# Gates and log-gate sums of a hybrid decoder step: one block of work cut into seven steps, and the cached sums in two wide matmuls

## The chip, the cores and the metric

One core of one Trainium2 chip runs the whole program. The metric is the device time of one execution in microseconds (us). A profiled execution gives a trace in which every instruction has a start, a length and, where its engine sat idle before it, what ended that idle time. The engines are PE (TensorE), ACT (ScalarE), DVE (VectorE), POOL (GpSimd) and SP, which issues most DMAs here. Each of them takes its instructions in a fixed order.

## The reference, cut to what matters

One layer serves a prompt of 1024 rows and 8 samples of 4 new rows, each sample with 1024 cached rows in 8 pages of 128. All matrices are float32. What bears on the change is the forget-gate side of the second head group (FoX), the branch gates of the first (NSA), and the projections around them:

```python
u = h @ w_in                                    # D = 1024, all head groups' columns side by side
logf = log_sigmoid(f_f + b_fgate)               # (b, t, 8 heads)
gates = sigmoid(g_n.reshape(b, t, KV_NSA, GRP, 3))
# prompt
c = cumsum(logf, axis=1)                        # 1024 rows
# samples
c_past = cumsum(gather_pages(cache_fox_logf, page_table, layer), axis=1)   # 8 samples x 1024 rows x 8 heads
c_new = c_past[:, -1:] + cumsum(logf, axis=1)
# both
logit = q . k * HEAD_DIM ** -0.5 + (cq - ck)    # then a masked softmax over the keys
...
cmp_kv = compress_blocks(kv_c, cmp_pos, w_cmp1, w_cmp2)   # NSA: an MLP over 32-row blocks of the cached rows
```

## The kernel before, in words

The normalised input lies transposed in eight tiles `ht`, split into a high and a low float32r half. A **projection** (`proj`, L227 to L246) makes 128 columns of `u` for all 1056 rows: it loads the weights in four DMAs (`wr`), ACT casts each to `wh` (L82), POOL subtracts to get `wl` (L83), and PE runs 72 matmuls of 352 columns (L243), 24 for each of three column chunks. Each chunk needs one PSUM tile of the tag `fl`, which has **two** buffers, and frees it when ACT or DVE has copied it out: for a q projection that copy is `os` (L509) on ACT.

A **compression chunk** (`cmp_chunk`, L422 to L485) takes two samples' pages (or, as the chunk `(NB,)`, the prompt's own rows in the tiles `cT`): transposes (L440, tags `sc` and `pt`), splits into tiles `X` (ACT L82, DVE L83), 48 matmuls for each of e = 0, 1 (L455, tags `pv` and `sv`; L460 for the prompt), a tanh (L472 on ACT, L473 and L474 on DVE) and a small product (L478). These tags are not `fl`.

`gates_and_sums` (L265 to L363) does the rest, all of it in `fl` tiles:

- L276: the projection for 24 gate and 8 forget columns, 48 matmuls, copied out to `gt`; L284 and L287 turn it to rows (`gf`).
- L291 to L322: tanh for the gates; Abs, Exp and Ln for the log-gates `lf`; seven additions for the prefix `pre` over the prompt's eight row blocks.
- L324, L325, L329: the prompt's cumulative sums, with a triangle of ones (`TRI`) and a full square of ones, copied out to `cn`, then turned and stored (`d_c`).
- L335 gathers the cached log-gates of 64 pages into `lp`; L343 turns them in eight transposes to `lpt`.
- L350 and L351: the cached cumulative sums. For each head, `lpt` of that head against `TRI`, and a 64x64 block matrix (`L64`) against the page totals `tot`, 16 matmuls of 128 columns in two PSUM tiles, then L353 and eight stores to `d_cs` (L355).
- L358 to L363: the sums for the new rows.

The program order around it is set by hand (L542 to L557): it is called once, after the chunk `(2, 3)` and a projection, and is followed by a projection, the chunk `(4, 5)`, two projections, the chunk `(NB,)` and the chunk `(6, 7)`. The framework's scheduler then fixes each engine's order with a model of its own: it may bring an instruction forward when its buffers allow, so the chunks' work, in other tags, stands among the gates' work, and the projections, in the same tag, stand behind it.

Much later `sam_fox` (L1156 to L1233) reads `d_cs` back as the tile `nk`, one DMA for four samples.

Of the kernel before, what the change touches and what calls it, by code (L numbers as in the profile page):

```python
# [25 lines left out]
TA = T + NS  # L26
# [5 lines left out]
      ("L64", 64), ("B64", 32), ("IMP", 16), ("IDX", 14), ("BM", 64), ("CM4", 4), ("WM4", 4), ("DG", 2)]  # L32
# [12 lines left out]
def tile_hymba_step(ctx: ExitStack, tc: tile.TileContext, I: dict, O: dict):  # L45
    nc = tc.nc

    def raw(t, off, dims):
        return bass.AP(tensor=t.tensor, offset=t.offset + off, ap=dims)
# [18 lines left out]
    def mm_tile(tag="fl"):  # L68
        return pst[1].tile([128, 512], F32, name="ps_" + tag, tag=tag, bufs=pst[2][tag])
# [20 lines left out]
    def evac(out, in_, scale=None):  # L90
        ev_n[0] += 1
        if scale is not None or ev_n[0] % 3:
            nc.scalar.activation(out, in_, AF.Copy, scale=1.0 if scale is None else scale)  # L93
        else:
            nc.vector.tensor_copy(out, in_)  # L95
# [39 lines left out]
    d_cs = dram.tile([NB, 8, 1024], F32, name="d_cs")  # L135
# [129 lines left out]
    def gates_and_sums():  # L265
        wg = gpool.tile([128, KD, 32], F32, name="wg")
        nc.sync.dma_start(wg[:, :, 0:24], w_in[:, 1280:1304].rearrange("(k p) c -> p k c", p=128))
        nc.sync.dma_start(wg[:, :, 24:32], w_in[:, 3352:3360].rearrange("(k p) c -> p k c", p=128))
        gt = lp_.tile([128, TA], F32, name="gt", tag="cT", bufs=3)
        for c in range(3):  # L270
            ps = mm_tile()
            s = slice(c * CH, (c + 1) * CH)
            for r in range(4):
                for q in range(4):
                    k = q + 4 * (r // 2)
                    nc.tensor.matmul(ps[32 * q:32 * q + 32, :CH], lhsT=wg[:, k], rhs=HT[k][:, r % 2, s].bitcast(F32),  # L276
                                     start=r == 0, stop=r == 3)
            evac(gt[:, s], ps[:, :CH])
        stk = cst[:, CO["STK"]]
# [17 lines left out]
        bf = gpool.tile([128, 8], F32, name="bf")  # L297
        nc.sync.dma_start(bf, raw(I["b_fgate"], 0, [[0, 128], [1, 8]]))
# [22 lines left out]
        for t in range(1, NT):  # L321
            nc.vector.tensor_add(pre[:, t], pre[:, t - 1], lf[:, t - 1])  # L322
        ps = mm_tile()
# [21 lines left out]
        cp = lp_.tile([128, TA], F32, name="cp", tag="cT", bufs=3)[:64, :1024].rearrange("p (h t) -> p h t", h=8)  # L345
        for h0 in (0, 4):
            ps = mm_tile()
            for h in range(4):
                o = ps[:64, h * 128:(h + 1) * 128]
                nc.tensor.matmul(o, lhsT=lpt[:, h0 + h], rhs=cst[:, CO["TRI"]], start=True, stop=False)  # L350
                nc.tensor.matmul(o, lhsT=cst[:64, CO["L64"]],  # L351
                                 rhs=tot[:, h0 + h:h0 + h + 1].to_broadcast([64, 128]), start=False, stop=True)
            nc.vector.tensor_scalar(cp[:, h0:h0 + 4], ps[:64].rearrange("p (h c) -> p h c", c=128), -1.0, None, op0=OP.mult)  # L353
        for b in range(NB):
            nc.sync.dma_start(d_cs[b].rearrange("h (g c) -> g h c", c=128), cp[b * 8:(b + 1) * 8])  # L355
# [131 lines left out]
    F0, F1, F2, F3, F4, F5 = 2, 1, 1, 2, 0, 0  # L487
# [37 lines left out]
    for e in range(2):  # L525
# [15 lines left out]
        pos.append(pT.rearrange("p (u j) -> p j u", u=2))  # L541
    cmp_chunk((0, 1), pgs)  # L542
    nsa_projections(F0)
# [3 lines left out]
    nsa_projections(F1)  # L547
    pgs = cmp_pages((4, 5))
    gates_and_sums()
    nsa_projections(F2)  # L550
    cmp_chunk((4, 5), pgs)
    nsa_projections(F3)
    pgs = cmp_pages((6, 7))
    cmp_chunk((NB,), None)
    nsa_projections(F4)
    cmp_chunk((6, 7), pgs)
    nsa_projections(F5)  # L557
# [598 lines left out]
    def sam_fox(gq):  # L1156
        bs = [gq * 4 + bl for bl in range(4)]
        nk = sp.tile([128, 1056], F32, name="nk", tag="s_l")[:, :1024]
        nc.sync.dma_start(nk, raw(d_cs, gq * 4 * 8192, [[1024, 32], [0, 4], [1, 1024]]))
# [259 lines left out]
def _consts():  # L1419
# [19 lines left out]
    l = np.zeros((128, 64))  # L1439
    l[:64] = (r[:, None] // 8 == r[None] // 8) & (r[:, None] % 8 < r[None] % 8)  # L1440
    c["L64"] = l
# [57 lines left out]
```

## Time and profile before

| | us |
|---|---|
| median of 3 runs | 1305.86 |
| lowest and highest run | 1299.7 and 1306.3 |
| the profiled execution | 1305.1 |
| its span, first to last instruction | 1303.3 |
| PE busy in it | 1206.6 |
| mean granted clock of TensorE (share of full) | 0.971 |

In the rows further down, PE is the matmul stream; one float32 matmul can show as two records (x2). "PEclk" is the share of TensorE's full clock of 2.4 GHz that was granted in a stretch: 1.00 is 2.4 GHz, 0.50 is 1.2 GHz, and values between are stretches with some of both. A text in brackets at the end of a timeline row is the idle time of the engine just before it and what ended it.

### The profile page before, as it was taken

The numbers are of one execution on the slowest core, as the hardware profiler recorded it, in microseconds if no ns is written. First come the engines' busy times: TensorE is split into PE (matmuls) and PEld (weight loads), VectorE is DVE, ScalarE is ACT, GpSimd is POOL, SyncE is SP. The second block draws the span as 40 slices with busy tenths as digits, with TensorE's granted clock in tenths as the row PEclk, the third lists the DMA queues.
The fourth block names the chain that finished last, engine by engine and source line by source line (L and its number), as shares of the span: only waits on it lengthen the run. The fifth ranks groups of instructions, "written<-read, shape, count | busy, mean of one in ns | idle before, by whom it ended". The sixth has DMA issues, their size and how long they took to land. (4 is left out here: it accounts for less than half of the span.)

```text
span 1303.3 us, 23755 instructions
## 1 busy us (share of the span) xinstructions
PE 1206.6 (93%) x8130; PEld 988.6 (76%) x8130; DVE 667.5 (51%) x2054; ACT 605.6 (46%) x1415; POOL 315.9 (24%) x433
## 2 busy tenths in 40 slices
PE   3899889999999999999889999999999787999998
PEld 3799669998989998989866666664664666877776
DVE  4614542434556566364368677665545746342222
ACT  7624433334455545453357676664555733131121
POOL 2411002022322222221132232222212433222112
PEclk8999969999999999999889999999999988999999
DMA  7434212047332223223552624546645465542221
GB/s 243 131 110 119 77 34 82 20 117 215 88 86 58 78 58 97 59 73 97 183 156 76 195 95 144 165 136 201 208 132 162 142 234 162 173 154 81 70 74 37
DMA packets 142747, 157.07 MB, mean 121 GB/s; under 512 B 16602, under 2 KB 109562, under 8 KB 142434
## 3 DMA queue, kind: packets, MB, share of 16 engines
q1 hardware_dynamic: 141394, 151.10, 37.7%
q10 hardware_dynamic: 1152, 4.19, 0.8%
q8 instruction: 64, 1.05, 0.3%
q14 instruction: 57, 0.47, 0.1%
q0 software_dynamic: 80, 0.26, 0.1%
HBM read 128.33 MB, written 36.38 MB: 126 GB/s over the span
## 5 line engine op out<-in xcount | busy, mean ns | idle before, releaser
L243 PE MATMUL ps_fl<-ht,wh 128*128 128x352 f32 x1440 | 367.0, 328 | 7.4 <-DVE os L498 3.6
L243 PEld LDWEIGHTS ps_fl<-ht,wh 128*128 128x128 f32 x1440 | 256.1, 190 | 12.4 <-DVE os L498 3.9
L243 PE MATMUL ps_fl<-ht,wl 128*128 128x352 f32 x720 | 236.3, 328 | 0.0
L620 ACT ACTIVATE s<-s,m 128x64 f32<-128x64 f32 (+8 forms) x256 | 164.4, 644 | 58.7 <-DVE m L618 55.6
L83 POOL TENSOR_TENSOR wl<-wr,wh 128x256 fp32r<-128x256 f32 x120 | 89.5, 750 | 267.7 <-ACT wh L82 266.7
L623 POOL TENSOR_SCALAR s<-s,rs 128x64 f32<-128x64 f32 (+8 forms) x160 | 93.4, 604 | 232.7 <-DVE rs L981 138.1
L243 PEld LDWEIGHTS ps_fl<-ht,wl 128*128 128x128 f32 x720 | 136.7, 190 | 1.1 <-issue 0.4
L638 PE MATMUL ps_pt<-cst,s 128*128 128x128 f32 x816 | 128.3, 284 | 3.3 <-POOL s L623 0.8
L612 PE MATMUL ps_sc<-kh,q 128*128 128x320 f32 (+12 forms) x304 | 116.4, 387 | 13.1 <-DVE m L618 7.0
L618 DVE CUSTOM_DVE_ANT_0 s<-ps_sc,bias 128x128 f32<-128x128 f32 (+10 forms) x224 | 80.3, 389 | 83.9 <-PE ps_sc L613 22.0
L638 PEld LDWEIGHTS ps_pt<-cst,s 128*128 128x128 f32 x816 | 97.8, 144 | 23.1 <-issue 6.0
L93 ACT ACTIVATE s<-ps_pt 128x512 f32<-128x512 f32 (+2 forms) x164 | 86.6, 539 | 57.3 <-PE ps_pt L638 45.4
L613 PE MATMUL ps_sc<-kl,q 128*128 128x320 f32 (+12 forms) x304 | 100.8, 335 | 1.5 <-DVE kl L601 1.5
L612 PEld LDWEIGHTS ps_sc<-kh,q 128*128 128x128 f32 x304 | 58.2, 191 | 46.5 <-DVE m L618 15.3
L618 DVE CUSTOM_DVE_ANT_0 s<-ps_sc,bias,m 128x320 f32<-128x320 f32 (+10 forms) x168 | 87.0, 523 | 7.3 <-PE ps_sc L613 3.4
L82 ACT CAST wh<-wr 128x256 fp32r<-128x256 f32 x120 | 47.8, 404 | 68.3 <-PE ps_fl L243 36.7
L95 DVE COPY s<-ps_pt 128x512 f32<-128x512 f32 (+2 forms) x84 | 49.9, 594 | 39.9 <-PE ps_pt L638 37.6
L748 POOL TENSOR_TENSOR mc<-bias,cst 128x128 f32<-128x128 f32 x64 | 30.2, 477 | 147.9 <-DVE m L618 136.1
L613 PEld LDWEIGHTS ps_sc<-kl,q 128*128 128x128 f32 x304 | 58.6, 193 | 3.8 <-issue 1.8
L626 DVE TENSOR_SCALAR s<-s,rs 128x128 f32<-128x128 f32 (+7 forms) x96 | 55.3, 604 | 1.9
L1283 PE MATMUL ps_sc<-fwh,xh 128*128 128x512 f32 x128 | 50.8, 397 | 2.1 <-ACT xh L82 2.1
L1283 PE MATMUL ps_sc<-fwl,xh 128*128 128x512 f32 x128 | 50.1, 391 | 0.0
(439 smaller groups left out, 2214.1 us busy)
## 6 DMA issues: line engine op xcount, KB each, us to landing
kp<-in_cache_fox_kv_dram SPq DMA_DIRECT2D x64, 256.0 KB
vp<-in_cache_fox_kv_dram SPq DMA_DIRECT2D x64, 256.0 KB
wr<-in_w_in_dram SPq DMA_DIRECT2D x120, 128.0 KB
pg<-in_cache_cmp_kv_dram SPq DMA_DIRECT2D x64, 128.0 KB
pg<-in_cache_slc_kv_dram SPq DMA_DIRECT2D x64, 128.0 KB
d_g<-d_r SPq DMA_DIRECT2D x1, 4800.0 KB
bias<-d_g SPq DMA_DIRECT2D x8, 520.0 KB
X<-in_x_prompt_dram SPq DMA_DIRECT2D x8, 512.0 KB
```

The costliest lines, as they stand in the source:

```text
L83: (l_eng or nc.vector).tensor_tensor(l, src, h.bitcast(F32), op=OP.subtract)
L93: nc.scalar.activation(out, in_, AF.Copy, scale=1.0 if scale is None else scale)
L95: nc.vector.tensor_copy(out, in_)
L243: nc.tensor.matmul(ps[:, :CH], lhsT=w[k // 2][:, k % 2], rhs=HT[k][:, hl, s], start=n == 0, stop=n == 3 * KD - 1)
L612: nc.tensor.matmul(out, lhsT=qi, rhs=ks[0][:, k0:k0 + n], start=True, stop=False)
L613: nc.tensor.matmul(out, lhsT=qi, rhs=ks[1][:, k0:k0 + n], start=False, stop=True)
L618: nc.vector.tensor_tensor_reduce(o, p, bi, scale=-1.0, scalar=BIG if x == 0 else m, op0=OP.add, op1=OP.min, accum_out=m)
L620: nc.scalar.activation(s_ap, s_ap, AF.Exp, scale=-1.0, bias=m, accum_out=ssum)
L623: nc.gpsimd.tensor_scalar(s_ap, s_ap, r, 0.0, op0=OP.mult, op1=OP.add)
L626: nc.vector.tensor_scalar(s_ap, s_ap, r, None, op0=OP.mult)
L638: nc.tensor.transpose(ps[:, (2 * x + a) * 128:(2 * x + a + 1) * 128], S[:, a, (b0 + x) * 128:(b0 + x + 1) * 128], ident)
L1283: nc.tensor.matmul(o, lhsT=a[al][:, k], rhs=w[k][wl][:, c * 512:(c + 1) * 512], start=k == 0 and x == 0, stop=k == nk - 1 and x == 2)
```

## The change

`gates_and_sums` becomes a generator with seven steps, and the calls that advance it stand between projections and chunks. Step 1 loads the weights and the bias; 2 is the gate projection (L276); 3 runs from L284 to the prefix additions; 4 is the prompt's sums, the gather, the transposes and a new prefix over the eight pages of a sample (seven additions of 64 columns in place of the block matrix); 5 makes the cached sums of all heads in two matmuls of 512 columns; 6 turns them in four transposes and stores them in one DMA; 7 is the sums for the new rows. One projection moves from ahead of the gates to a place after step 2, and the six projections of this stage now stand one by one. `d_cs` has the heads ahead of the samples, so `nk` is loaded by four DMAs. The constant `L64` goes.

```diff
@@ -29,7 +29,7 @@
 KD = D // 128
 
 _w = [("ID", 128), ("TRI", 128), ("CM", 128), ("WM", 128), ("STK", 32), ("DM", 8), ("RM", 1), ("GM", 128), ("BT", 32),
-      ("L64", 64), ("B64", 32), ("IMP", 16), ("IDX", 14), ("BM", 64), ("CM4", 4), ("WM4", 4), ("DG", 2)]
+      ("B64", 32), ("IMP", 16), ("IDX", 14), ("BM", 64), ("CM4", 4), ("WM4", 4), ("DG", 2)]
 CO = {}
 C_ALL = 0
 for _n, _k in _w:
@@ -132,7 +132,7 @@
     d_g = dram.tile([128, 8, RW], F32, name="d_g")
     d_sb = dram.tile([32, 1028], F32, name="d_sb")
     d_c = dram.tile([8, T], F32, name="d_c")
-    d_cs = dram.tile([NB, 8, 1024], F32, name="d_cs")
+    d_cs = dram.tile([8, NB, 1024], F32, name="d_cs")
     d_cn = dram.tile([NB, 8, 4], F32, name="d_cn")
     d_gs = dram.tile([NS, 24], F32, name="d_gs")
 
@@ -266,6 +266,9 @@
         wg = gpool.tile([128, KD, 32], F32, name="wg")
         nc.sync.dma_start(wg[:, :, 0:24], w_in[:, 1280:1304].rearrange("(k p) c -> p k c", p=128))
         nc.sync.dma_start(wg[:, :, 24:32], w_in[:, 3352:3360].rearrange("(k p) c -> p k c", p=128))
+        bf = gpool.tile([128, 8], F32, name="bf")
+        nc.sync.dma_start(bf, raw(I["b_fgate"], 0, [[0, 128], [1, 8]]))
+        yield
         gt = lp_.tile([128, TA], F32, name="gt", tag="cT", bufs=3)
         for c in range(3):
             ps = mm_tile()
@@ -276,6 +279,7 @@
                     nc.tensor.matmul(ps[32 * q:32 * q + 32, :CH], lhsT=wg[:, k], rhs=HT[k][:, r % 2, s].bitcast(F32),
                                      start=r == 0, stop=r == 3)
             evac(gt[:, s], ps[:, :CH])
+        yield
         stk = cst[:, CO["STK"]]
         gf = gpool.tile([128, NT + 1, 32], F32, name="gf")
         nc.vector.memset(gf[:, NT], 0.0)
@@ -294,8 +298,6 @@
         nc.sync.dma_start(d_gs, gat_s)
         nc.vector.tensor_scalar(gates[:, 0, 0:24:3], gates[:, 0, 0:24:3], cst[:, CO["RM"]], None, op0=OP.mult)
 
-        bf = gpool.tile([128, 8], F32, name="bf")
-        nc.sync.dma_start(bf, raw(I["b_fgate"], 0, [[0, 128], [1, 8]]))
         f1 = gpool.tile([128, NT + 1, 8], F32, name="f1")
         f2 = gpool.tile([128, NT + 1, 8], F32, name="f2")
         f3 = gpool.tile([128, NT + 1, 8], F32, name="f3")
@@ -320,6 +322,7 @@
         nc.vector.memset(pre[:, 0], 0.0)
         for t in range(1, NT):
             nc.vector.tensor_add(pre[:, t], pre[:, t - 1], lf[:, t - 1])
+        yield
         ps = mm_tile()
         nc.tensor.matmul(ps[:, :64], lhsT=cst[:, CO["TRI"]], rhs=lf[:, :NT], start=True, stop=False)
         nc.tensor.matmul(ps[:, :64], lhsT=ones, rhs=pre, start=False, stop=True)
@@ -342,17 +345,28 @@
         for h in range(8):
             nc.tensor.transpose(ps[:, h * 64:(h + 1) * 64], lp[:, :, h], ident[:64, :64])
         nc.vector.tensor_copy(lpt, ps.rearrange("p (h c) -> p h c", c=64))
-        cp = lp_.tile([128, TA], F32, name="cp", tag="cT", bufs=3)[:64, :1024].rearrange("p (h t) -> p h t", h=8)
-        for h0 in (0, 4):
-            ps = mm_tile()
-            for h in range(4):
-                o = ps[:64, h * 128:(h + 1) * 128]
-                nc.tensor.matmul(o, lhsT=lpt[:, h0 + h], rhs=cst[:, CO["TRI"]], start=True, stop=False)
-                nc.tensor.matmul(o, lhsT=cst[:64, CO["L64"]],
-                                 rhs=tot[:, h0 + h:h0 + h + 1].to_broadcast([64, 128]), start=False, stop=True)
-            nc.vector.tensor_scalar(cp[:, h0:h0 + 4], ps[:64].rearrange("p (h c) -> p h c", c=128), -1.0, None, op0=OP.mult)
-        for b in range(NB):
-            nc.sync.dma_start(d_cs[b].rearrange("h (g c) -> g h c", c=128), cp[b * 8:(b + 1) * 8])
+
+        ca = lp_.tile([128, TA], F32, name="ca", tag="cT", bufs=3)
+        pgc = ca[:, 512:1024].rearrange("p (h b g) -> p h b g", b=NB, g=8)
+        lv = lpt.rearrange("p h (b g) -> p h b g", g=8)
+        nc.vector.memset(pgc[:, :, :, 0], 0.0)
+        for g in range(1, 8):
+            nc.vector.tensor_tensor(pgc[:, :, :, g], pgc[:, :, :, g - 1], lv[:, :, :, g - 1], op=OP.add)
+        yield
+        ps = mm_tile()
+        nc.tensor.matmul(ps, lhsT=cst[:, CO["TRI"]], rhs=lpt.rearrange("p h c -> p (h c)"), start=True, stop=False)
+        nc.tensor.matmul(ps, lhsT=ones, rhs=pgc.rearrange("p h b g -> p (h b g)"), start=False, stop=True)
+        ca = ca[:, :512]
+        nc.vector.tensor_scalar(ca, ps, -1.0, None, op0=OP.mult)
+        yield
+        ps = mm_tile()
+        for x in range(4):
+            nc.tensor.transpose(ps[:, x * 128:(x + 1) * 128], ca[:, x * 128:(x + 1) * 128], ident)
+        cp = lp_.tile([128, TA], F32, name="cp", tag="cT", bufs=3)[:, :512]
+        nc.vector.tensor_copy(cp, ps)
+        nc.sync.dma_start(d_cs.rearrange("h b (g c) -> (h b g) c", c=128).rearrange("(x p) c -> p x c", p=128),
+                          cp.rearrange("p (x c) -> p x c", c=128))
+        yield
 
         ps = mm_tile()
         nc.tensor.matmul(ps[:8, :NS], lhsT=tot, rhs=cst[:64, CO["B64"]], start=True, stop=False)
@@ -484,7 +498,6 @@
             else:
                 nc.vector.tensor_copy((kcp, vcp)[e], pv2[:, 0])
 
-    F0, F1, F2, F3, F4, F5 = 2, 1, 1, 2, 0, 0
     def out_stage():
         return cp_.tile([128, CH], F32, name="os", bufs=2)
 
@@ -539,22 +552,30 @@
         pT = cp_.tile([128, 16], F32, name="posT", bufs=2)
         nc.vector.tensor_copy(pT, ps[:, :16])
         pos.append(pT.rearrange("p (u j) -> p j u", u=2))
+    G = gates_and_sums()
+    next(G)
     cmp_chunk((0, 1), pgs)
-    nsa_projections(F0)
+    nsa_projections(1)
     pgs = cmp_pages((2, 3))
     cmp_proj(1)
     cmp_chunk((2, 3), pgs)
-    nsa_projections(F1)
+    nsa_projections(1)
     pgs = cmp_pages((4, 5))
-    gates_and_sums()
-    nsa_projections(F2)
+    next(G)
+    nsa_projections(1)
+    next(G)
     cmp_chunk((4, 5), pgs)
-    nsa_projections(F3)
+    nsa_projections(1)
+    next(G)
     pgs = cmp_pages((6, 7))
     cmp_chunk((NB,), None)
-    nsa_projections(F4)
+    nsa_projections(1)
+    next(G)
     cmp_chunk((6, 7), pgs)
-    nsa_projections(F5)
+    next(G)
+    nsa_projections(1)
+    for _ in G:
+        pass
     qst.close()
 
 
@@ -1156,7 +1177,8 @@
     def sam_fox(gq):
         bs = [gq * 4 + bl for bl in range(4)]
         nk = sp.tile([128, 1056], F32, name="nk", tag="s_l")[:, :1024]
-        nc.sync.dma_start(nk, raw(d_cs, gq * 4 * 8192, [[1024, 32], [0, 4], [1, 1024]]))
+        for bl in range(4):
+            nc.sync.dma_start(nk[32 * bl:32 * bl + 32], raw(d_cs, bs[bl] * 1024, [[8192, 8], [0, 4], [1, 1024]]))
         n4 = sp.tile([128, 4], F32, name="n4", bufs=2)
         nc.sync.dma_start(n4, raw(d_cn, gq * 128, [[4, 32], [0, 4], [1, 4]]))
         nc.vector.tensor_tensor(n4, n4, cst[:, CO["CM4"]], op=OP.add)
...
```

How the orders move, at three places. First **PE, from the prompt's sums to the cached sums**. Before, from L325 on (`cn`: the copied prompt sums; `lp`, `lpt`: cached log-gates; `pg`: page rows being turned for a chunk):

```order
L325 MATMUL ps_fl<-pre,ones 128x64 [waits DVE_49]
L440 MATMUL ps_sc<-cst,pg 128x128 [waits DMAHW4_49,DMAHW3_49]
L329 MATMUL ps_fl<-cst,cn 64x128 [waits DVE_49]
L343 MATMUL ps_fl<-cst,lp 128x64 [waits DMASW0_49,PE_49]
L343 MATMUL ps_fl<-cst,lp 128x64 x7
L440 MATMUL ps_sc<-cst,pg 128x128 [waits DMAHW6_49,DMAHW5_49]
L350 MATMUL ps_fl<-cst,lpt 64x128 [waits DVE_49]
L351 MATMUL ps_fl<-tot,cst 64x128
```

In the changed kernel (its own line numbers: L454 is L440 before, L327, L328, L332 and L346 are L324, L325, L329 and L343, L492 is L478, L469 is L455):

```order
L454 MATMUL ps_sc<-cst,pg 128x128 [waits DMAHW5_49,DMAHW4_49]
L454 MATMUL ps_sc<-cst,pg 128x128 [waits DMAHW7_49,DMAHW6_49]
L327 MATMUL ps_fl<-lf,cst 128x64 [waits Activation_49]
L328 MATMUL ps_fl<-pre,ones 128x64 [waits DVE_49]
L332 MATMUL ps_fl<-cst,cn 64x128 [waits DVE_49]
L346 MATMUL ps_fl<-cst,lp 128x64 [waits DMASW0_49,Activation_49]
L346 MATMUL ps_fl<-cst,lp 128x64 x7
L492 MATMUL ps_pv<-th,w_674 64x128 [waits DVE_49]
L492 MATMUL ps_pv<-th,w_674 64x128
L469 MATMUL ps_sv<-X,w1h 128x258 [waits Activation_49]
L469 MATMUL ps_sv<-X,w1l 128x258
L243 MATMUL ps_fl<-ht_111,wh 128x352 [waits DVE_49]
```

The sixteen narrow matmuls are gone from here and projection matmuls (L243) follow. Ahead of these rows stand 27 more L243, the end of the projection set after step 3, and ahead of those the chunk's product on tag `pv`. L327 now waits for ACT.

The same place **on ACT**, before (from the last page casts of a chunk on; `cT`: the prompt's rows, cast for the chunk `(NB,)`; L472: its tanh's table and tanh; L509: copies of a projection):

```order
L82 CAST X<-cT 64x8x64 x4
L82 CAST X<-posT 128x8x2 [waits PE_49]
L82 CAST X<-cT 64x8x64 x4
L82 CAST X<-ps_pt 64x8x64 [waits PE_49]
L472 ACT_TABLE_LOAD
L472 ACTIVATE th<-ps_pv,bt 128x256 [waits DVE_49]
L82 CAST X<-ps_pt 64x8x64 [waits DVE_49]
L509 ACTIVATE os<-ps_fl 128x352 [waits DMAHW7_49,PE_49]
L509 ACTIVATE os<-ps_fl 128x352 [waits DMAHW5_49,PE_49]
L82 CAST wh<-wr 128x256 [waits DMAHW3_49,PE_49,Pool_49]
```

and in the changed kernel (L486 is L472, L522 is L509):

```order
L82 CAST X<-ps_sc 64x8x64 [waits DVE_49]
L82 CAST X<-posT 128x8x2 [waits PE_49,Activation_49]
L82 CAST X<-cT 64x8x64 x4
L82 CAST X<-posT 128x8x2 [waits PE_49]
L82 CAST X<-cT 64x8x64 x4
L82 CAST X<-ps_pt 64x8x64 [waits PE_49]
L486 ACT_TABLE_LOAD
L486 ACTIVATE th<-ps_pv,bt 128x256 [waits DVE_49]
L522 ACTIVATE os<-ps_fl 128x352 [waits DMAHW6_49,PE_49]
L82 CAST wh<-wr 128x256 [waits DMAHW4_49,PE_49,Pool_49]
```

The casts and the tanh keep their order. The copy L522 right behind the tanh empties the middle chunk of the projection whose last chunk stands ahead of L327 on PE. Before, the two copies L509 belonged to a projection that stands behind the whole block on PE.

Last, **PE at steps 5 and 6** of the changed kernel (`ca`: prefix, then the sums; L357 and L358: the two wide matmuls; L364: the transposes):

```order
L243 MATMUL ps_fl<-ht_118,wh 128x352
L357 MATMUL ps_fl<-lpt,cst 128x512 [waits DVE_49]
L358 MATMUL ps_fl<-ca,ones 128x512
L454 MATMUL ps_pt<-cst,pg 128x128
L454 MATMUL ps_sc<-cst,pg 128x128 x4
L454 MATMUL ps_pt<-cst,pg 128x128 x4
L454 MATMUL ps_sc<-cst,pg 128x128 x4
L492 MATMUL ps_sv<-th,w_700 64x64 [waits DVE_49,PE_49]
L492 MATMUL ps_sv<-th,w_700 64x64
L364 MATMUL ps_fl<-cst,ca 128x128 [waits DVE_49]
L364 MATMUL ps_fl<-cst,ca 128x128 x3
L243 MATMUL ps_fl<-ht_111,wh 128x352
```

These stand between whole thirds of projections, where before there was nothing of the gates.

## Rows read from the trace of the kernel before

**Rows 1.** Page, part 1: busy time of each engine, its share, instructions.

```profile
PE 1206.6 (93%) x8130; PEld 988.6 (76%) x8130; DVE 667.5 (51%) x2054; ACT 605.6 (46%) x1415; POOL 315.9 (24%) x433
```

**Rows 2.** Windows: length, busy (instructions) of PE, PEld, DVE, ACT, POOL, PEclk, DMA, GB/s.

```profile
150.00:155.00 5.00, 2.42 (x11) 2.03 (x12) 3.69 (x8) 4.80 (x10) 0.83 (x1) 0.75 0.73 192
155.00:160.00 5.00, 5.00 (x40) 5.00 (x40) 4.79 (x9) 1.35 (x3) 0.00 (x0) 0.90 0.27 75
160.00:165.00 5.00, 2.98 (x23) 2.37 (x22) 4.63 (x20) 4.57 (x7) 0.00 (x0) 1.00 0.19 32
165.00:170.00 5.00, 2.56 (x12) 1.61 (x12) 4.84 (x8) 4.89 (x7) 0.00 (x0) 0.62 0.27 80
170.00:175.00 5.00, 3.99 (x14) 2.00 (x14) 3.86 (x6) 2.26 (x3) 0.00 (x0) 0.50 0.04 10
175.00:180.00 5.00, 5.00 (x18) 2.29 (x16) 1.77 (x3) 0.00 (x0) 0.00 (x0) 0.50 0.00 0
180.00:185.00 5.00, 5.00 (x25) 3.65 (x24) 1.15 (x3) 0.00 (x0) 0.00 (x0) 0.50 0.23 43
185.00:190.00 5.00, 5.00 (x31) 5.00 (x31) 0.00 (x0) 0.00 (x0) 0.00 (x0) 0.83 0.11 23
```

**Rows 3.** Timeline of PE, 136 to 181 us: start, length, instruction, idle time and releaser.

```profile
136.23 2.57 PE L276 MATMUL ps_fl<-ht,wg 128*32 128x352 f32 x32
...
147.26 0.60 PE L440 MATMUL ps_pt<-cst,pg 128*128 128x128 f32 x4
...
152.12 0.39 PE L455 MATMUL ps_pv<-X,w1h 128*128 128x258 f32 x1 [2.46 <-ACT X L82]
...
166.59 0.45 PE L440 MATMUL ps_sc<-cst,pg 128*128 128x128 f32 x1 [2.82 <-DMA pg<-in_cache_cmp_kv_dram]
...
171.01 0.69 PE L350 MATMUL ps_fl<-cst,lpt 128*64 128x128 f32 x2 [1.86 <-DVE lpt L344]
...
180.26 0.69 PE L351 MATMUL ps_fl<-tot,cst 64*64 64x128 f32 x2
```

**Rows 4.** Timeline of PE: the same three-matmul group (L455) at either clock, then L243.

```profile
154.71 0.63 PE L455 MATMUL ps_pv<-X,w1h 128*128 128x258 f32 x2
...
155.35 0.63 PE L455 MATMUL ps_pv<-X,w1h 128*128 128x258 f32 x2
...
156.35 0.40 PE L455 MATMUL ps_pv<-X,w1h 128*128 128x258 f32 x2
...
156.71 0.40 PE L455 MATMUL ps_pv<-X,w1h 128*128 128x258 f32 x2
...
187.37 0.48 PE L243 MATMUL ps_fl<-ht,wh 128*128 128x352 f32 x2
...
187.85 0.48 PE L243 MATMUL ps_fl<-ht,wh 128*128 128x352 f32 x2
```

**Rows 5.** Timeline of DVE: the prefix additions of the prompt.

```profile
161.94 1.15 DVE L322 TENSOR_TENSOR pre<-pre,lf 128x8 f32<-128x8 f32 x6
```

**Rows 6.** Timeline of ACT, 160 to 192 us.

```profile
160.49 0.21 ACT L82 CAST X<-posT 128x16 fp32r<-128x16 f32 x1 [0.34 <-PE ps_pv L455]
...
169.92 1.28 ACT L472 ACT_TABLE_LOAD   x1
171.22 0.47 ACT L472 ACTIVATE th<-ps_pv,bt 128x256 f32<-128x256 f32 x1
...
191.08 0.47 ACT L509 ACTIVATE os<-ps_fl 128x352 f32<-128x352 f32 x1 [16.76 <-PE ps_fl L243]
```

**Rows 7.** Timeline of SP (page loads), then of PE (their first transposes).

```profile
59.88 10.71 SPq L148 DMA_DIRECT2D pg<-in_cache_cmp_kv_dram  x15
...
106.81 0.60 PE L440 MATMUL ps_sc<-cst,pg 128*128 128x128 f32 x4
```

**Rows 8.** Tile nk: its loads and its readers, first and last start.

```profile
L1159 SPq DMA_DIRECT2D nk<-d_cs x2: 561/566/571, 764.2 to 911.7; - x2
...
L1195 DVE CUSTOM_DVE_ANT_0 s_s<-ps_sv,nk x2: 424/425/426, 826.6 to 927.8; 128x256 f32<-128x256 f32 x2
```

More of the change, by code (lines that the diff above doesn't have):

```diff
@@ L1438, in _consts @@
     r = np.arange(64)
-    l = np.zeros((128, 64))
-    l[:64] = (r[:, None] // 8 == r[None] // 8) & (r[:, None] % 8 < r[None] % 8)
-    c["L64"] = l
     l = np.zeros((128, 32))
```

## The prediction

> **What bounds the kernel.** I read the page's busy times first: PE is busy 93% of the span, the next engine, DVE, 51% [rows 1]. So PE's own time and the holes in it make the time, and a change off PE counts only if it makes or closes a hole. The windows by stretch come next, because the share is an average. PE runs full on either side of the gates, but from 150 to 190 us it has holes and a low clock [rows 2]. Idle time is 5 us less the busy time of a window: 2.58 + 2.02 + 2.44 + 1.01 = 8.05 us (150, 160, 165 and 170). The granted clock falls to 0.75 after PE sat idle 2.46 us, comes back, and falls to 0.50 around an idle time of 2.82 us; it is full again only near 187 [rows 2, 3]. Read as time at 1.2 GHz, a window with share s has (1 - s) x 2 x 5 us of it: 2.5, 1.0, 3.8, 5, 5, 5 and 1.7 us, in which PE was busy about 2.4 + 1.0 + 2.6 + 14.0 + 1.7 = 21.7 us. What that costs is seen where the same three matmuls ran at either level: they start 0.64 us apart at 1.2 GHz and 0.36 us apart at 2.4 GHz [rows 4], so 0.44 of the slow busy time is lost, 9.5 us. **The block loses 8.05 + 9.5 = 17.6 us.**
>
> The timeline says why nothing fills the holes. The projection that comes next in the program starts at 187 us, behind the whole block: its PSUM tiles have the gates' tag, with two buffers. What PE finds instead is the chunks' work, and that waits too, for ACT's casts, for pages and for DVE's copy of the turned log-gates [rows 3].
>
> **The change, part by part.** The sum is made against the profiled execution, 1305.1 us, 0.8 us under the median of 1305.86; I carry no correction for that.
>
> *The sixteen narrow matmuls go.* L350 and L351 run from 171.01 to 180.95 us [rows 3], 9.9 us, all at 1.2 GHz. Of these 0.44 are in the 9.5 above, so 0.56 x 9.9 = 5.6 us at full clock go. In their place come two matmuls of 512 columns and four transposes. The trace has no such float32 matmul, so I bound it. From below: L276's 32 records of 352 columns take 2.57 us with four quarters of the array side by side, hence 0.32 us for a full-array record, two records a matmul: 512/352 x 0.64 x 2 = 1.9 us. From above: the narrow records take 9.9/32 = 0.31 us for 128 columns at 1.2 GHz, 0.17 at full clock: x 4 x 2 x 2 = 2.8 us. I take 1.9, since a long pass at full clock is what they are. Four transposes take 0.60 [rows 3]. Net 5.6 - 2.5 = **3.1 us gained** (2.2 at the upper end).
>
> *The block is cut.* Three projections come to stand among its steps: 72 matmuls each, 0.16 us apart [rows 4], 11.5 us a projection. The chain from L284 to the prefix additions, in which PE stood idle 2.46 us, lies beside one of them and a chunk's product. The holes of 17.6 us go, as far as the new order closes them.
>
> *One wait opens.* On PE, L327 now stands behind a projection, and it waits for ACT, because the PSUM buffer it takes is that of the projection's middle chunk. On ACT that copy stands behind ten casts for the prompt's chunk, a page cast, a table load and a tanh. Before, this same chain ran from 160.49, when PE ended the chunk's product, to 171.69 (the tanh's end) [rows 6]; the copy adds 0.47, together 11.7 us from the product's end. In the changed order PE has 27 projection matmuls and 16 transposes to do in that time: 27 x 0.16 + 16 x 0.15 = 6.7 us. **So PE sits idle 5.0 us at L327.** Behind it on PE stand L328, L332, L346 and the next projection; nothing overtakes. A hole of 2.5 us cost the clock before, so I let it fall again: after that first hole it came back within 3.5 us of time at 1.2 GHz, after the second only after some 20 [rows 2]. A projection stands behind L346, as a chunk's product stood behind the first hole, so I take 3 to 8 us of slow work, 0.44 of it lost, 1.3 to 3.5 us; I take 2.4. L346 needs the projection's last copy, which comes after three weight casts on ACT; the turning of the sums runs in that time. For this, the chunk's wait for casts and the last pages (the 2.82 us wait of [rows 3], now with a third of a projection in front) I put 1.0. New losses: 5.0 + 2.4 + 1.0 = **8.4 us**.
>
> [...]
>
> *What lies beside other work.* The seven additions over pages have 64 columns; L322 takes 1.15/6 = 0.19 us for 8 [rows 5], so 1.4 us at the least, and twice that changes nothing: the two wide matmuls that need them come after a projection and both products of the prompt's chunk. Without that cover they would cost their 1.4 to 3. DVE's copies are as many as before. Eight stores become one, with SP free there. The weights' and the bias's loads go out ahead of some compression weights; those have the first chunk's transposes in front, and I count nothing, 1 us at worst. The projection moved away from the front leaves 11.5 us less cover for the pages of the second chunk, but these are issued from 59.9 to 70.6 and first used at 106.8 [rows 7]: still 25 us. Six more loads of `nk` at 0.57 us are 3.4 us on SP; `nk` was loaded 62 and 16 us ahead of its first readers [rows 8].
>
> **Sum:** 17.6 + 3.1 - 8.4 = 12.3 us gained, 1305.1 - 12.3 = **1293 us**. Behind the block the order on PE stays the same but for some steps of the samples, so I expect the gain to reach the end.
>
> **Rivals.**
>
> *No wait at L327.* If ACT gets through its casts earlier, only the small waits stay: 17.6 + 3.1 - 1.0 = 19.7, 1285. For it: ACT is busy only 46% of the span [rows 1]. Against: its casts for the prompt's chunk cannot begin before the product on `pv` releases the tile they write [rows 6]. Chance 0.16.
>
> *A second wait of the same size,* at L357 or at L364, where DVE has a chunk's splits in front of the gates' small work: 12.3 - 7.4 = 4.9, 1300. For it: a shared engine order is just what makes the first wait. Against: the projections in front are whole ones there. Chance 0.12.
>
> *Slower.* The two-buffer ring that held the projections behind the gates now makes each step's copy a wait of a projection. Places are L327, L357, L364 and the new rows' sums, each worth 5.0 + 2.4 = 7.4 us. From three on the gain of 19.7 is used up (22.2); with all four it is 19.7 - 29.6 = -9.9, 1315. For it: ACT and DVE serve projections, chunks and gates in one order. Against: at the later places the order shows one gate instruction each, with no table load in front. [...] Chance 0.05.
>
> *The change does not reach the end:* a later stage waits for something that did not move, a transfer say, and the time is 1304 to 1306. For it: PE is full for long stretches, so a hole may open unseen. Against: its loads are issued in step with PE's own progress, so they move along. Chance 0.09.
>
> **How the numbers follow.** The forecast has 0.58, with 1290 to 1298 as its own spread (slow work 3 or 8 us, wide matmuls 2 or 3, small waits 0 to 3). 0.5%, about 6.5 us, is what a measurement of this kernel can tell from no change, so faster means under 1298.6: 0.55 of the forecast's 0.58, 0.16 of the no-wait case and 0.03 of the second-wait case, 0.74. Slower by that much needs all four places: 0.05. The rest, 0.21, is no change. The range goes from the no-wait case, 1285, to the second-wait case with a little noise, 1301; that leaves out 0.14 and some noise.
>
> **What would show it.** Right: L350 and L351 gone, two matmuls of 512 columns at about 1 us each; projection matmuls between 146 and 190 us; one idle time of PE near 5 us at L327, released by ACT, with the clock at 1.2 GHz for some us behind it; the windows before and behind it full. Wrong: no idle time there, or more than one of that size; a clock that stays low for 20 us as before; or the gates gone by 12 us earlier and the end not.

## The result and the profile after

The changed kernel takes 1293.54 us, median of 7 runs (1289.5 to 1296.01), against 1305.86 for the kernel before beside it (7 runs): the ratio is 0.9899, with a 95% interval of 0.9878 to 0.992. That is 12.3 us by the medians. The forecast was 1293, in a range of 1285 to 1301, with 0.74 on faster by over 0.5%; the time lies 0.5 us above the forecast. The profiled execution of the changed kernel is the fastest of its seven, 1289.5 us with a span of 1287.7, so what is compared with the one before is the stretch around the change and not its end.

The busy times first, page, part 1 (before: [rows 1]):

```profile
PE 1194.4 (93%) x8106; PEld 981.2 (76%) x8106; DVE 670.0 (52%) x2062; ACT 604.1 (47%) x1415; POOL 312.8 (24%) x433
```

PE has 24 records fewer and 12.2 us less busy time; all other engines are within 1% of what they were. The gain is thus PE's own: less slow time, the narrow matmuls' work, and fewer holes beside it. The windows of the same stretch as in [rows 2] (columns as there):

```profile
150.00:155.00 5.00, 5.00 (x34) 5.00 (x33) 4.36 (x6) 4.37 (x8) 0.00 (x0) 1.00 0.83 213
155.00:160.00 5.00, 5.00 (x42) 4.98 (x41) 4.74 (x12) 1.32 (x3) 0.00 (x0) 1.00 0.26 82
160.00:165.00 5.00, 5.00 (x39) 5.00 (x38) 3.49 (x16) 2.67 (x4) 0.00 (x0) 1.00 0.27 55
165.00:170.00 5.00, 3.40 (x26) 3.14 (x24) 4.74 (x7) 4.90 (x6) 0.00 (x0) 1.00 0.19 60
170.00:175.00 5.00, 0.95 (x4) 0.93 (x4) 3.13 (x5) 4.92 (x10) 0.63 (x1) 0.74 0.02 8
175.00:180.00 5.00, 4.68 (x23) 3.75 (x23) 4.20 (x13) 1.24 (x3) 2.22 (x4) 0.50 0.59 161
180.00:185.00 5.00, 5.00 (x29) 5.00 (x28) 0.55 (x2) 0.00 (x0) 0.00 (x0) 0.74 0.10 24
185.00:190.00 5.00, 5.00 (x45) 5.00 (x43) 0.70 (x6) 0.99 (x3) 0.00 (x0) 1.00 0.01 3
```

The hole at 150 us with its fall of the clock is gone, and so are the 20 us at 1.2 GHz behind the second one. One hole is left, and behind it (1 - s) x 10 = 2.6, 5 and 2.6 us at 1.2 GHz, 10.2 in all against 24.0 before; PE worked in about 0.95 + 4.7 + 2.6 = 8.2 us of it.

The records of the clock in this trace and in that of the kernel before have the shares 0.50 and 1.00 and none between. In this trace matmuls of 352 columns (L243, 178 to 182 us) start 0.293 us apart at 0.50, and those of 512 (L1314, 1071 to 1076 us) 0.427: 1.20 columns a ns both. At 1.00 the two widths start 0.161 (L243, 163 to 167 us) and 0.227 us apart (L1305, 1274 to 1276 us), so 160 columns more take 0.066 us, 2.4 a ns. The 1.2 and 2.4 GHz of this text are an estimate by these rates, with one column to a clock.

The timeline of PE shows what the hole is, and the new sums of the heads:

```profile
174.04 0.69 PE L327 MATMUL ps_fl<-lf,cst 128*128 128x64 f32 x2 [5.64 <-ACT os L522]
174.53 0.63 PE L328 MATMUL ps_fl<-pre,ones 128*128 128x64 f32 x2
175.48 0.69 PE L332 MATMUL ps_fl<-cst,cn 128*64 128x128 f32 x2 [0.32 <-DVE cn L330]
...
205.75 1.02 PE L357 MATMUL ps_fl<-lpt,cst 128*128 128x512 f32 x2
206.61 1.02 PE L358 MATMUL ps_fl<-ca,ones 128*128 128x512 f32 x2
...
209.25 0.66 PE L364 MATMUL ps_fl<-cst,ca 128*128 128x128 f32 x4
```

PE sat idle 5.64 us at L327, released by ACT's copy `os` (L522, a projection's copy out of PSUM). It is the only wait of PE over 0.4 us between 100 and 260 us. L357 and L358 take 1.88 us together from start to end, the four transposes 0.66. ACT's timeline ahead of that copy:

```profile
162.28 0.21 ACT L82 CAST X<-posT 128x16 fp32r<-128x16 f32 x1 [2.71 <-PE ps_pv L469]
162.40 4.42 ACT L82 CAST X<-cT 64x512 fp32r<-64x512 f32 x4
166.85 0.21 ACT L82 CAST X<-posT 128x16 fp32r<-128x16 f32 x1
166.96 4.29 ACT L82 CAST X<-cT 64x512 fp32r<-64x512 f32 x4
171.27 0.58 ACT L82 CAST X<-ps_pt 64x512 fp32r<-64x512 f32 x1
171.87 1.28 ACT L486 ACT_TABLE_LOAD   x1
173.16 0.47 ACT L486 ACTIVATE th<-ps_pv,bt 128x256 f32<-128x256 f32 x1
173.54 0.46 ACT L522 ACTIVATE os<-ps_fl 128x352 f32<-128x352 f32 x1
```

Eight casts of `cT` (the prompt's chunk, 64 x 512 each) take 8.7 us, and the copy that PE wants is behind them, a page cast, a table load and the tanh. PE had used up its other work at 168.40.

### The profile page after: what moved, and what is told of

The parts are those of the page before. It is cut to its first block, busy times and chain, and to the rows that moved or that the text cites. A ratio compares the mean times of both kernels' runs of the same rounds, so it can differ in the third digit from the quotient of the medians.

```text
span 1287.7 us, 23713 instructions
## 1 busy us (share of the span) xinstructions
PE 1194.4 (93%) x8106; PEld 981.2 (76%) x8106; DVE 670.0 (52%) x2062; ACT 604.1 (47%) x1415; POOL 312.8 (24%) x433
## 3 DMA queue, kind: packets, MB, share of 16 engines
q8 instruction: 64, 1.05, 0.3%
## 5 line engine op out<-in xcount | busy, mean ns | idle before, releaser
L243 PE MATMUL ps_fl<-ht,wh 128*128 128x352 f32 x1440 | 368.0, 329 | 5.6 <-DVE os L511 3.7
L243 PEld LDWEIGHTS ps_fl<-ht,wh 128*128 128x128 f32 x1440 | 256.6, 191 | 10.5 <-DVE os L511 4.0
L243 PE MATMUL ps_fl<-ht,wl 128*128 128x352 f32 x720 | 236.7, 329 | 0.0
L83 POOL TENSOR_TENSOR wl<-wr,wh 128x256 fp32r<-128x256 f32 x120 | 89.1, 748 | 261.1 <-ACT wh L82 258.1
L243 PEld LDWEIGHTS ps_fl<-ht,wl 128*128 128x128 f32 x720 | 137.0, 190 | 1.1 <-issue 0.4
L633 PEld LDWEIGHTS ps_sc<-kh,q 128*128 128x128 f32 x304 | 58.5, 192 | 50.5 <-DVE m L639 17.6
L1305 PE MATMUL ps_sc<-fwh,xh 128*128 128x512 f32 x128 | 50.8, 397 | 2.1 <-ACT xh L82 2.1
L1305 PE MATMUL ps_sc<-fwl,xh 128*128 128x512 f32 x128 | 50.1, 391 | 0.0
```

Source lines behind the costliest of these rows:

```text
L83: (l_eng or nc.vector).tensor_tensor(l, src, h.bitcast(F32), op=OP.subtract)
L243: nc.tensor.matmul(ps[:, :CH], lhsT=w[k // 2][:, k % 2], rhs=HT[k][:, hl, s], start=n == 0, stop=n == 3 * KD - 1)
L633: nc.tensor.matmul(out, lhsT=qi, rhs=ks[0][:, k0:k0 + n], start=True, stop=False)
L1305: nc.tensor.matmul(o, lhsT=a[al][:, k], rhs=w[k][wl][:, c * 512:(c + 1) * 512], start=k == 0 and x == 0, stop=k == nk - 1 and x == 2)
```

## The experiments

Nine kernels were run. Those of one set share the runs of the kernel before on their chip: the first four (before: 1304.01 us), then e5 to e7 (1305.6), then e8 and e9 (1304.79). The last column, the stretch, is read from the one profiled execution of each: from the first matmul of the first chunk's product to the first score matmul of the prompt's FoX heads, between which nearly all of the change stands (not the loads of weights, bias and `nk`). Before and in the changed kernel these are:

```profile
58.58 0.39 PE L455 MATMUL ps_pv<-X,w1h 128*128 128x258 f32 x1 [0.50 <-ACT X L82]
...
297.97 0.30 PE L612 MATMUL ps_sc<-kh,q 128*128 128x128 f32 x1
```

```profile
57.61 0.39 PE L469 MATMUL ps_pv<-X,w1h 128*128 128x258 f32 x1 [0.51 <-ACT X L82]
...
284.61 0.30 PE L633 MATMUL ps_sc<-kh,q 128*128 128x128 f32 x1
```

That is 239.4 us before and 227.0 in the changed kernel, 12.4 less. The stretch comes out alike in two profiles of one kernel (227.0 and 227.1 for the changed kernel and e7, 218.0 and 217.7 for e6 and e9). What lies ahead of it ended between 56.4 and 59.9 us over all eleven profiles, and what comes after it took 1003 to 1010 us; that scatter is in the medians too.

| run | what it is | median us | ratio to before, 95% interval | stretch, us |
|---|---|---|---|---|
| e1 | steps spread, old narrow sums | 1295.55 | 0.9933 (0.9908 to 0.9958) | 230.4 |
| e2 | wide sums, steps in one piece | 1304.59 | 0.9995 (0.9976 to 1.0014) | 235.6 |
| e3 | after, last two chunks exchanged | 1291.22 | 0.9884 (0.9856 to 0.9913) | 227.1 |
| e4 | after, without the logarithm's table | 1290.93 | 0.9883 (0.9858 to 0.9909) | 225.6 |
| e5 | after, four casts of cT on POOL | 1291.66 | 0.9893 (0.9856 to 0.9930) | 226.0 |
| e6 | after, eight casts of cT on POOL | 1285.09 | 0.9837 (0.9800 to 0.9873) | 218.0 |
| e7 | after again | 1293.57 | 0.9909 (0.9877 to 0.9941) | 227.1 |
| e8 | before, eight casts of cT on POOL | 1304.18 | 0.9987 (0.9967 to 1.0008) | 233.4 |
| e9 | e6 again | 1282.98 | 0.9824 (0.9795 to 0.9853) | 217.7 |

### The two halves of the change

**e1**, the spread alone: the old sums are put back, each half of them as a step of its own, with their eight stores and the one load of `nk`.

```diff
-        ca = lp_.tile([128, TA], F32, name="ca", tag="cT", bufs=3)
...
-        nc.tensor.matmul(ps, lhsT=cst[:, CO["TRI"]], rhs=lpt.rearrange("p h c -> p (h c)"), start=True, stop=False)
...
+        for h0 in (0, 4):
+            yield
+            ps = mm_tile()
+            for h in range(4):
+                o = ps[:64, h * 128:(h + 1) * 128]
...
```

> The changed kernel, but with the old sums of the heads (sixteen matmuls with a 128-column result each, eight stores, one load of nk): only the setting of the steps between projections is left of the change. Theory (the holes and the low clock of the old block were the loss): the sixteen matmuls now run between projections with the clock at full, where they cost about 5.6 us by half of the 9.9 us that they took at 1.2 GHz, against the 2.5 us of the two wide matmuls and four transposes; so about 3 us above the changed kernel, 1296 to 1297, and some 9 us below the kernel before. PE shows the same single wait at the first sum matmul (L327) and no idle at L350/L351. Rival (the sixteen narrow matmuls and their eight stores were the loss): within 3 us of the kernel before, 1303 or more.

**e2**, the wide sums alone: the steps keep the place that they had before, and the projections too.

```diff
-    nsa_projections(1)
+    nsa_projections(2)
...
-    next(G)
+    for _ in G:
+        pass
...
```

> The other half alone: the two wide matmuls, the four transposes, the one store and the four loads of nk of the changed kernel, but all steps in one piece at the place that they had before. Theory: the holes of the block stay (8 us idle and the low clock), the new prefix over g on VectorE and the turn of the result add waits of their own to it, and what is gained is 9.9 us of narrow matmuls at 1.2 GHz less about 5 us of wide ones and transposes at 1.2 GHz: 1299 to 1305, if the prefix (seven additions of about 0.1 to 0.15 us) and two more copies from PSUM (about 0.5 us each) stand open in the row, nearer to the upper end. Rival (the arithmetic carries the gain): within 2 us of the changed kernel, about 1294.

e1 came to 1295.55 us, at 0.9933, and e2 to 1304.59, at 0.9995, both within about 1 us of the theory. So the spread carries about two thirds of the gain by itself (8.5 us), and the wide sums by themselves carry none that the medians show. What the wide sums add to the spread is too small for the times, whose intervals overlap (0.9908 to 0.9958 in e1, 0.9878 to 0.992 in the changed kernel); it is read from the traces. In e1 PE's two largest waits are those of the changed kernel:

```profile
PE ps_fl L327 <- ACT os L514: 5.6, 1, 5.6
PE ps_fl L332 <- DVE cn L330: 0.3, 1, 0.3
```

and half of the sixteen narrow matmuls, at full clock, runs like this, 205.44 to 208.40 us:

```profile
205.44 0.43 PE L355 MATMUL ps_fl<-cst,lpt 128*64 128x128 f32 x2
205.80 0.43 PE L356 MATMUL ps_fl<-tot,cst 64*64 64x128 f32 x2
...
207.97 0.43 PE L356 MATMUL ps_fl<-tot,cst 64*64 64x128 f32 x2
```

One pair starts 0.72 us after the other, so the eight pairs of both halves take 5.8 us, against 1.88 + 0.66 = 2.5 in the changed kernel: 3.3 us saved, and the stretch of e1 is 230.4 - 227.0 = 3.4 us longer. That these agree so well is in part chance, for the same hole cost e1 less of the clock:

```profile
170.00:175.00 5.00, 0.90 (x4) 0.90 (x4) 3.09 (x5) 4.92 (x10) 0.57 (x1) 0.85 0.01 4
175.00:180.00 5.00, 4.68 (x24) 3.72 (x24) 2.61 (x7) 1.31 (x3) 2.27 (x4) 0.50 0.60 164
180.00:185.00 5.00, 5.00 (x37) 5.00 (x36) 0.00 (x0) 0.00 (x0) 0.00 (x0) 0.96 0.11 25
```

These are 1.5 + 5 + 0.4 = 6.9 us at 1.2 GHz against 10.2 in the changed kernel, about 1 us less lost. In e2 the holes of the block are still there, as its waits from 100 to 260 us show, of which these are the largest:

```profile
PE ps_pv L469 <- ACT X L82: 2.5, 1, 2.5
PE ps_sc L454 <- DMA pg<-in_cache_cmp_kv_dram: 2.2, 1, 2.2
PE ps_fl L357 <- DVE lpt L347: 2.0, 1, 2.0
PE ps_sv L469 <- ACT X L82: 1.3, 1, 1.3
```

The wait on `lpt` that stood ahead of the narrow matmuls [rows 3] stands ahead of the wide one, and a wait of 1.3 us is new. Behind its first hole the clock stayed at 1.2 GHz for 6.8 us (shares of 0.99, 0.50 and 0.83 from 150 to 165 us), where it was 3.5 before [rows 2]:

```profile
155.00:160.00 5.00, 4.50 (x21) 4.50 (x22) 3.77 (x6) 2.48 (x4) 0.00 (x0) 0.50 0.52 144
```

Even so the stretch of e2's profiled execution is 235.6 us, 3.8 less than in the one trace of the kernel before, and its median does not show that. Whether other executions lose it, or this one trace of the kernel before is long, stays open.

### What the new order still loses

**e3** exchanges the last two compression chunks, so that the casts of cT come later.

```diff
     pgs = cmp_pages((6, 7))
-    cmp_chunk((NB,), None)
+    cmp_chunk((6, 7), pgs)
     nsa_projections(1)
     next(G)
-    cmp_chunk((6, 7), pgs)
+    cmp_chunk((NB,), None)
```

> The changed kernel with the order of the last two compression chunks exchanged, so that the ten casts of cT (9.2 us of ScalarE ahead of the copy that the matmul at L327 waited for) come later in ScalarE's order. Theory (the one wait of 5.6 us at L327, and the stretch of about 10 us at 1.2 GHz behind it, are what the new order still loses, and ScalarE's casts are the cause): both go, 5.6 us of idle and about 4 us of low clock, so 1284 to 1286; if a smaller wait takes their place at the later chunk, up to 1289. Rival (the wait is set by something else, such as the tanh and its table load, or moves whole to the other chunk): 1291 to 1295, with a PE wait of 4 us or more elsewhere in 160 to 230 us.

The rival won: 1291.22 us, which the intervals do not tell from the changed kernel. The wait is gone from L327, and the same casts make one of nearly the same size 29 us later, now through VectorE (DVE): its step L511 of a z projection needs ACT's tanh of it, which stands behind the casts.

```profile
202.68 2.08 PE L357 MATMUL ps_fl<-lpt,cst 128*128 128x512 f32 x2 [5.35 <-DVE os L511]
```

The wait belongs to the casts of cT and not to a place in the order.

**e4** takes the logarithm's table out of ACT's chain.

```diff
-        nc.scalar.activation(f4, f3, AF.Ln)
+        nc.scalar.activation(f4, f3, AF.Exp)
```

> The changed kernel with an exponential in place of the logarithm in the log-gates (the logarithm is left out, so the log-gates and all that follows from them have other values); the order on every engine is the same, but the two table loads of this stage, 1.28 us each, are gone, one of them (ahead of the tanh at L486) in the chain that the matmul at L327 waits for. By the rows (the tanh starts 0.01 us after the load's end): the wait shrinks from 5.6 to 4.3 us, or to about 3 if the first load pushed the casts too, and the time goes down by 1.3 to 4 us, the latter if the clock does not fall any more. [...] Rival (the wait at L327 does not hang on ScalarE's chain): the wait stays at 5.6 us and the time within 1 us of the changed kernel.

The wait went from 5.64 to 4.38 us, by 1.26 us, the length of one load (1.28):

```profile
PE ps_fl L327 <- ACT os L522: 4.4, 1, 4.4
```

So it does hang on ACT's chain, microsecond for microsecond. The tanh started 1.31 us after the page cast's end in the changed kernel (171.85 to 173.16), and 0.02 us after it without the load. The shorter wait did not shorten the time at 1.2 GHz (10.3 us), the stretch is 1.4 us shorter than in the changed kernel, and the time, 1290.93 us, is not told from the changed kernel's.

**e5** and **e6** take the casts themselves off ACT, four of them (e = 1) and all eight; **e7** is the changed kernel beside them.

```diff
-                        split(dv[0], dv[1], sv)
+                        if b == NB and e == 1:
+                            nc.gpsimd.tensor_copy(dv[0], sv)
+                            nc.vector.tensor_tensor(dv[1], sv, dv[0].bitcast(F32), op=OP.subtract)
+                        else:
+                            split(dv[0], dv[1], sv)
```

(e6 has `if b == NB:` there.)

> The changed kernel with four of the eight long casts of cT (those of the second half, e = 1, 4.3 us on ScalarE) on GpSimd, which is idle there for 25 us; nothing else is changed. In the exchange of the chunks the wait had only moved with these casts, so they are taken off ScalarE itself. Theory (every us of these casts that is ahead of the copy os on ScalarE is a us of the wait at L327): the wait falls from 5.6 us by 4.3 to about 1.3 us, the clock falls for a shorter stretch or not at all, and the time is 4 to 8 us below the changed kernel. Rival (another chain of about the same length stands behind it, through VectorE's subtractions or GpSimd's own late casts): a wait of 3 us or more stays at L327 or appears at L332, L346 or the cT chunk's matmuls (ps_pv<-X 128x260), and the time is within 2 us of the changed kernel.

> All eight casts of cT on GpSimd. Theory: the copy os comes 1.28 (table load) + 0.47 + 0.46 us after the tanh's input, at about 165 us, before TensorE needs it at 168.4, so no wait at L327, no low clock in 165 to 190 us, and 6 to 10 us below the changed kernel (5.6 us of idle and about 4 us of low clock). Rival (GpSimd takes several times as long as ScalarE for such a cast, 8 casts of 1.1 us become over 25 us): the cT chunk's matmuls, which start at 188.9 us now, wait for the casts, or the projections wait for the splits of the weights (wl) behind them on GpSimd, and the gain is half or nothing.

> The changed kernel itself once more, on the same chip as the two runs beside it, so that they are compared with it and not only with the kernel before: 1290 to 1296 us, a wait of 5.6 us at L327 and nothing else in 100 to 260 us, the clock at its lower level for some 10 us behind it.

e5 came 1.9 us below e7, within what the rival gave, and its waits show why. The one at L327 falls by 4 us as the theory said, but the order on PE changes with it, and the chunk's product (L473, `ps_sv`) and the matmul that follows the tanh (L496) find their inputs late:

```profile
PE ps_sv L473 <- ACT X L82: 2.3, 1, 2.3
PE ps_fl L327 <- ACT os L526: 1.6, 1, 1.6
PE ps_pv L496 <- DVE qsam L529: 1.1, 1, 1.1
```

Three holes of 5.0 us in all stand for one of 5.6, and the clock falls again, for 6.9 us. Of the 4.0 us by which the wait at L327 fell, 3.4 came back at the other two. The rival's chain through VectorE can be seen: beside GpSimd's casts three of its subtractions took 1.76 us each, where they take 1.10 in the changed kernel, and the page cast on ACT that L473 waits for was itself held by VectorE.

```profile
164.80 5.29 DVE L83 TENSOR_TENSOR X<-cT,X 64x512 fp32r<-64x512 f32 x3
...
173.53 0.58 ACT L82 CAST X<-ps_pt 64x512 fp32r<-64x512 f32 x1 [1.21 <-DVE X L83]
```

How much of the two new holes comes from this slowing was not measured apart.

e6 came 8.5 us below e7 (1285.09 against 1293.57; the intervals of the two ratios do not meet). The trace shows no wait of PE at all in 100 to 260 us. Two windows of what was the hole:

```profile
165.00:170.00 5.00, 5.00 (x39) 4.54 (x39) 4.94 (x5) 2.23 (x6) 4.76 (x5) 1.00 0.36 118
170.00:175.00 5.00, 5.00 (x42) 4.69 (x41) 4.61 (x8) 0.69 (x2) 4.85 (x5) 1.00 0.05 13
```

and the timeline of ACT from the table load on:

```profile
163.04 1.28 ACT L490 ACT_TABLE_LOAD   x1
164.34 0.47 ACT L490 ACTIVATE th<-ps_pv,bt 128x256 f32<-128x256 f32 x1
164.71 0.46 ACT L526 ACTIVATE os<-ps_fl 128x352 f32<-128x352 f32 x1
```

The copy that PE waited for until 174.0 is over at 165.2. The stretch is 9.1 us shorter than in e7 (9.4 in e9), which is about what the hole cost: 5.6 + 0.3 us idle and 0.44 x 8.2 = 3.6 us of low clock make 9.5 in the changed kernel. GpSimd takes 10.16 us for the eight casts, 1.27 each against ACT's 1.1, and PE never waits for them:

```profile
161.92 10.16 POOL L463 CAST X<-cT 64x512 fp32r<-64x512 f32 x8 [12.94 <-PE ps_pv L473]
```

This version beats both kernels; e9 confirms it with 1282.98 us.

### Are the two losses one?

**e8** puts the casts of the kernel before on GpSimd, with nothing of the change (the edit is that of e6).

> The kernel before, with nothing of the change, but with the eight casts of cT on GpSimd. It asks whether the two losses, that of the old block and that which the new order kept, are one and the same. Theory (the old block's holes come from its chain of dependent steps with nothing between, and the casts only lengthen one of them): of the waits of before in 150 to 190 us the 2.5 us on ScalarE's X go, those on a page's transfer (2.8), on lpt (1.9) and on sn (1.1) stay, the clock still falls, and the time is 2 to 5 us below the kernel before, 1300 to 1303. Rival (the burst of casts on ScalarE is behind both losses: without it the chunk's matmuls are ready early and stand between the block's steps by themselves, as the order on TensorE, which now has 41 matmuls of ps_sv between L343 and L350, allows): the holes of 170 to 181 us go with their low clock, the narrow matmuls run at full clock, and the time is 10 to 14 us below, 1291 to 1295.

> The changed kernel with all eight casts of cT on GpSimd once more, beside the run above: about 1285 us, no wait of TensorE above 0.5 us in 100 to 260 us and the clock at its upper level there. If the run above comes to within 3 us of it, the spread steps and the wide matmuls are worth little once the casts are off ScalarE; if it stays 10 us or more above, they are worth about what the change gained.

1304.18 us, at 0.9987: no gain that can be measured, just above the theory's 1300 to 1303 and far from the rival's 1291 to 1295. The largest waits from 100 to 260 us are those of a chain with too little between its steps:

```profile
PE ps_pv L459 <- ACT X L82: 2.5, 1, 2.5
PE ps_sc L440 <- DMA pg<-in_cache_cmp_kv_dram: 1.3, 1, 1.3
PE ps_fl L329 <- DVE cn L327: 1.1, 1, 1.1
```

The theory was right on the time and wrong on the waits. The 2.5 us on ACT's `X`, which were to go, stayed: they stand at 152 us [rows 3], ahead of the casts of `cT` (from 160.6 us on in the kernel before), and are on casts of pages. The page wait, which was to stay, fell from 2.8 to 1.3 us, and the 1.9 us on `lpt` went. Much of the rival was seen instead: the chunk's product does come ahead of L350 now, the narrow matmuls run at full clock (5.9 us, 175.88 to 181.74), and most of the 20 us at 1.2 GHz is gone, so that the stretch is 6 us shorter in its profiled execution. That execution is the fastest of twelve, though (1297.68 us, the others up to 1308.55), and their median does not keep the 6 us. Where the other executions lose them was not profiled and stays open. With the steps spread the same edit is worth 8.5 us and more, and e9 is 21.2 us below e8 where the change alone gained 12.3, so the two losses are not one: in these kernels moving the casts paid only once the other holes were closed.

## Why the prediction was right

**The block's loss and where the spread puts it.** The prediction put 17.6 us on holes and low clock and said that cover by projections closes the holes. e1 shows that this alone gives most of the gain, and e2 that without it the median shows none. The hole of 2.46 us at the chunk's casts and that at the pages are gone, the windows from 150 to 165 us are full.

**The narrow matmuls.** 5.6 us at full clock against 2.5, net 3.1 gained, was the term. e1 shows 5.8 us, the changed kernel 1.88 + 0.66: net 3.3. The lower bound was the right one for the 512 columns (1.9 us).

**The wait at L327.** It was forecast at 5.0 us, released by ACT, behind ten casts, a page cast, a table load and a tanh. It is 5.64, by that chain: 162.28 to 174.0, the 11.7 us that the term had. The other side was 0.5 us off: PE's cover was 6.2 us (162.16 to 168.40) and not 6.7, since the sixteen transposes start 0.11 us apart there, not 0.15. e4 and e6 show that the chain on ACT is the cause. The table load weighs in it with its own length: without the load of 1.28 us the wait is 1.26 us shorter (e4).

**The clock behind it.** 2.4 us was the term (1.3 to 3.5); 8.2 us of slow work at 0.44 are 3.6, at the upper bound. This is the term that was mis-sized. It is no fixed price either: behind the same wait of 5.6 us e1 lost about 6.0 x 0.44 = 2.6.

**Small waits.** 1.0 us was put, 0.32 came: the wait at L332.

**The sum.** By these rows 17.6 + 3.3 - 5.6 - 0.3 - 3.6 = 11.4 us are gained where 12.3 were forecast. The medians show 12.3, the stretch 12.4. Of the 1.0 us between, 0.3 is the part of the first hole that lies ahead of 150 us: it is 2.46 us long and ends at 152.12, and the sum of 8.05 began at 150. The other 0.7 is in none of the terms and was not found. Wait and clock were put 1.8 us too low, and the small waits, the narrow matmuls and what was not in the sum made up for it, so the near hit is in part luck.

**The rivals.** No wait at L327 would have been 1285; the wait is there, and e6, where it is not, came to 1285.09 and 1282.98: that rival's price was right, its condition was not met. No second wait of that size came at L357 or L364; e3 shows that one does come at L357 once the casts are moved there, with 5.35 us, so its mechanism was real as well. The slower case needed waits at three places or more; there is one. The changed kernel's projections use their two buffers in turn from 185 to 260 us, and PE is busy in 75.00 of these 75 us, with the clock at 1.00.

**Hidden work.** The seven prefix additions (L354) took 2.35 us, 178.23 to 180.58, between my 1.4 and twice that, and L357 did not wait for them. The eight loads of `nk` make no wait of PE.

## What to carry to other kernels

In this kernel a chain of small dependent steps cost PE its holes, 8.05 us, and then again 9.5 us by the low clock behind them; set such steps between pieces of full work, and look for the copies that those pieces need on the engine that was idle in the chain before. When the order of one engine then holds up one such copy (5.64 us here, behind 8.7 us of casts), find the long burst in front of it and move all of it to an idle engine (e6, no wait left): moving its place (e3, a wait of 5.35 us) or half of it (e5, 3.4 of 4.0 us came back) mostly moved the wait. Each edit alone, wide sums (e2) or casts on GpSimd (e8), gave nothing that the median shows while other holes were left, and about 3 us (by the traces) and 9 us once they were closed, so a null result in a stretch with several holes does not show that an edit is worthless.

## What was unexpected of the hardware

**The same hole costs the clock differently.** Behind a hole of 2.46 us at the same place, the windows from 150 to 165 us add up to 3.5 us at 1.2 GHz before, 6.8 in e2 and 6.8 in e8. The hole of 5.6 us at L327 left PE at 1.2 GHz for 10.2 us in the changed kernel and in e7, but for 6.9 in e1; a shorter one of 4.4 us in e4 for 10.3, and three of 5.0 in all in e5 for 6.9. So the length of a hole alone did not set what it cost the clock. The two kernels with all their holes vary by 9 us (e2, 1298.15 to 1307.17) and 11 us (e8) over twelve executions; those without holes there by 6 us (e6) and 3 us (e9) over six. Whether the uneven clock causes that scatter was not tried.

**VectorE slows beside GpSimd's casts.** While GpSimd cast `cT` in e6, some of VectorE's small instructions took several times as long; the first row is from just before the casts began to tell, the next two beside them, each a 16-column piece of work that takes 0.17 us in the changed kernel:

```profile
161.89 0.18 DVE L446 CAST X<-zero 128x16 fp32r<-128x16 f32 x1 [0.37 <-PE ps_pv L473]
162.17 0.86 DVE L446 CAST X<-zero 128x16 fp32r<-128x16 f32 x1
163.10 1.05 DVE L83 TENSOR_TENSOR X<-posT,X 128x16 fp32r<-128x16 f32 x1
...
165.32 1.91 DVE L464 TENSOR_TENSOR X<-cT,X 64x512 fp32r<-64x512 f32 x1
```

and VectorE's subtraction of a cast took 1.91 us there against 1.05 at 173.3 us, when GpSimd's casts were over. VectorE's subtractions that read PSUM (L83, `X<-ps_pt,X`) took 0.69 and 0.70 us beside the casts (164.18 and 167.65 us), as in the changed kernel (0.68). In e6 the slowing cost nothing, since PE had other work; in e5 the chain to the new holes ran through it. The three delays, 0.69, 0.88 and 0.86 us, are each shorter than one cast (1.27 us); what causes them no run here shows.
